# Expert weights in blocks of 256 rows by 1024 columns: two sums from each block, another order of small steps, and a table moved to the third expert

## The chip, the cores and the metric

The kernel runs on one core of one Trainium2 chip. The metric is the device time of one execution in microseconds (us). The time before is 1823.71 us, the median of three runs (1822.42 to 1827.42).

## The reference

The program is one layer of a trunk: a token mixer (Fourier groups beside retention heads), then an expert feed-forward stage, then a last normalisation. The change lies in the expert stage:

```
logits = h @ router_w + router_b            # 1024 tokens, 32 experts
top_vals, top_idx = top_k(logits, 4)
gates = softmax(top_vals)
for each expert e, over the tokens xb that chose it:
    hb    = xb @ w1[e] + b1[e]              # w1[e]: 1024 x 2048, float32
    x_glu = minimum(hb[:, ::2], 7)
    x_lin = clip(hb[:, 1::2], -7, 7)
    act   = x_glu * sigmoid(1.702 * x_glu) * (x_lin + 1)
    out   = act @ w2[e] + b2[e]             # w2[e]: 1024 x 1024
y[token] += gate * out
```

The weights of all 32 experts are 403 MB of float32, read once.

## The kernel before

The mixer takes the first part of the span; from about 540 us on the expert stage runs, and behind it the tail (normalisation of the sums).

**Experts and blocks.** Experts are ordered by load. CAPS[r] is the number of token columns n reserved for rank r; large and small ones alternate (132, 130, 134, 128, 136, ... 176, 91, 192, 84). Experts with n above 128 have two row blocks of tokens, of 128 and n - 128 rows. A weight matrix is cut into blocks of 512 rows by 512 columns (1 MB). An expert has twelve, and twelve steps t = 0 to 11, one block each. q = 0 to 3 are the column quarters of w1, q = 4 and 5 the halves of w2, s = 0 and 1 the upper and the lower 512 rows. The order is (0,0), (0,1), (1,0), (1,1), (2,0), (2,1), (3,0), (3,1), (4,0), (5,0), (4,1), (5,1).

**A step.** `block` (L1418) issues the block's load on SyncE's queue into one of ten `raw` tiles (NRAW). `lower` (L1426) computes on VectorE the remainder of each weight against its upper 16 bits and puts it, as float16, into one of six `lo` tiles (NLO). `product` (L1435) issues 48 matrix products of n columns: 32 with the upper halves of `raw` ("the upper part"), then 16 with `lo` ("the lower part"). The step of u issues `lower` for block u + 4 (AHEAD) and the load of block u + 10, which takes the buffer that step u has freed.

**The small steps between.** The loop at L1373 writes the order out by hand. After step u's product come, in this order: the loads, `lower(u + 4)`, the stages of `swiglu` or `yout` that are pending (L1391), the pending `rest` of a row transpose (L1397), and the next piece of `side` (L1398). `swiglu` has three stages with ScalarE and VectorE taking turns: L1479 to L1482, L1486, L1490 to L1492. At t = 8 all its pending stages run at once. `side` is `finish(r - 1)` from t = 0 (results transposed back, L1338 and L1341, then an indirect DMA into `acc`, L1343) and `turn(r + 1)` from t = 7 (the next expert's gathered token rows transposed, L1459). A piece of `turn` writes one of two `px` banks; its `rest` empties the bank with two ScalarE copies (L1464, L1465) and one VectorE remainder (L1466). With n above 128 there are three pieces, so the third needs the first one's bank.

**Selection and routing.** `select` (L1264) makes, in one VectorE instruction, the 0/1 matrix `sel` that picks an expert's tokens; `batch` (L1271) multiplies it with `aux` on TensorE at t = 5 of every even r, for experts r + 2 and r + 3, and VectorE turns the result into row indices (L1290 to L1298). `gather` (L1306) fetches the rows with an indirect DMA on GpSimd's queue. `routing` (L1079) is a generator; its last two parts run at t = 3 and t = 5 of r = 0 and make the table of surplus token blocks (`tab`, `tabi`) that `overflow` reads. With these inputs the loop of `overflow` runs no time.

Of the kernel before, what the change touches and what calls it, by code (L numbers as in the profile page):

```python
# [9 lines left out]
F32 = mybir.dt.float32  # L10
# [27 lines left out]
NRAW, NLO, AHEAD = 10, 6, 4  # L38
# [69 lines left out]
class K:  # L108
# [23 lines left out]
    def build(self):  # L132
        nc, tc, T = self.nc, self.tc, self.T
        with ExitStack() as es:
# [28 lines left out]
            self.tab = dram.tile([128, 4], F32, name="tab")  # L163
            self.tabi = dram.tile([128, 1], I32, name="tabi")
# [912 lines left out]
    def routing(self, rp):  # L1077
# [150 lines left out]
    def experts(self, routing):  # L1228
# [6 lines left out]
        U = [(r, q, s) for r in range(NE) for q, s in STEPS]  # L1235
        raw, low, info, B, X, A, Y, pss = {}, {}, {}, {}, {}, {}, {}, {}
# [4 lines left out]
        def load(u):  # L1241
            r, q, s = U[u]
            if u % 12 == 0:
                reg[r] = nc.sync.value_load(self.eid[0:1, r:r + 1], min_val=0, max_val=NE - 1)
                B[r] = self.es_.tile([128, 24], F32, name="bias", bufs=3)
            raw[u] = self.block(reg[r], q, s)
            if u % 12 == 0:
                nc.sync.dma_start(B[r], self.biasd[:, bass.ds(reg[r], 1), :].rearrange("p a j -> p (a j)"))
# [7 lines left out]
        def lower(u):  # L1256
            if u < len(U):
                low[u] = self.lower(raw[u])
# [95 lines left out]
        sels[0] = select(0, sel)  # L1354
# [6 lines left out]
        sels[1] = select(1)  # L1361
# [11 lines left out]
        for u, (r, q, s) in enumerate(U):  # L1373
# [23 lines left out]
            run(rest)  # L1397
# [20 lines left out]
    def block(self, e, q, s):  # L1418

        src = self.T["expert_w1" if q < 4 else "expert_w2"][0][bass.ds(e, 1)].rearrange("a (k p) n -> (a p) k n", p=128)  # L1420
        c0 = 512 * (q % 4)
        raw = self.wp.tile([128, 4, 512], F32, name="raw", bufs=NRAW)
        self.nc.sync.dma_start(raw, src[:, 4 * s:4 * s + 4, c0:c0 + 512])
        return raw

    def lower(self, raw):  # L1426

        lo = self.wp.tile([128, 4, 512], F16, name="lo", bufs=NLO)
# [5 lines left out]
    def product(self, ps, raw, lo, s, x, n, pairs):  # L1434


        nc = self.nc
        if pairs:

            up = raw.bitcast(BF).rearrange("p k (c m g h) -> p k c g m h", c=2, g=2, h=2)[:, :, :, :, :, 1]  # L1440
            dn = lo.rearrange("p k (c m g) -> p k c g m", c=2, g=2)
        else:
            up = raw.bitcast(BF).rearrange("p k (c g m h) -> p k c g m h", c=2, g=2, h=2)[:, :, :, :, :, 1]
            dn = lo.rearrange("p k (c g m) -> p k c g m", c=2, g=2)
        for w, parts in ((up, (0, 1)), (dn, (2,))):
            for c in range(2):
                for g in range(2):
                    o = ps[:, c, g * n:g * n + n]
                    for k in range(4):
                        for i in parts:  # L1450
                            nc.tensor.matmul(o, w[:, k, c, g, :], x[:, 4 * s + k, i, :], start=not (s or i or g or k), stop=s == 1 and i == 2 and k == 3, skip_group_check=True)  # L1451
# [52 lines left out]
    def expert(self, n, e, fetched, bias):  # L1504
# [3 lines left out]
        def sums(q, x):  # L1508
            ps = self.ph.tile([128, 2, 512], F32, name="ph")
            for s in range(2):  # L1510
                raw = self.block(e, q, s)
                self.product(ps, raw, self.lower(raw), s, x, n, q < 4)
            return ps

        act = self.ep.tile([128, 8, 3, n], F16, name="act", bufs=1)
        for q in range(4):
            for st in self.swiglu(sums(q, xT), q, act, n, bias):
                st()
        yT = self.ep.tile([128, 8, n], F32, name="yT", bufs=1)
        for q in range(4, 6):  # L1520
            for st in self.yout(sums(q, act), 4 * (q - 4), yT, n, bias):
                st()
# [30 lines left out]
    def overflow(self):  # L1553
# [3 lines left out]
        with tc.For_i(0, cnt, 1) as b:  # L1557
            par = self.es_.tile([128, 4], F32, name="par")
            nc.sync.dma_start(par, self.tab[bass.ds(b, 1), :].to_broadcast([128, 4]))
            ei = self.es_.tile([1, 1], I32, name="ei")  # L1560
            nc.sync.dma_start(ei, self.tabi[bass.ds(b, 1), :])
# [40 lines left out]
```

## Time and profile before

| | us |
|---|---|
| median of three runs | 1823.71 |
| the profiled execution | 1822.8 |
| its span, first to last instruction | 1820.9 |
| TensorE busy in the span | 1693.6 |
| VectorE busy | 1489.6 |
| ScalarE busy | 654.6 |
| GpSimd busy | 252.0 |

The profile is of one execution. Times in its rows count from the start of the span. PE is TensorE's matrix products, PEld its weight loads, DVE is VectorE, ACT ScalarE, POOL GpSimd, SP SyncE. An instruction's idle time stands behind it in brackets with what ended it. The DMA share is the mean busy share of the 16 DMA engines; it goes a little over 1 where packets overlap. PEclk is the granted TensorE clock: 1.00 is 2.4 GHz, 0.50 is 1.2 GHz.

### The profile page before, as it was taken

The page shows a single profiled execution, that of the slowest core. Times are in us where ns is not written, and L with a number is a line of the kernel's source. Part 1 is how long each engine was busy: PE and PEld are TensorE (multiplying, and loading weights), DVE is VectorE, ACT ScalarE, POOL GpSimd, SP SyncE. Part 2 cuts the span into 40 slices and gives each one's busy share as a digit, 9 for nine tenths or more (in the row PEclk, how much of TensorE's full clock was granted, in tenths as well). Part 3 has the DMA queues.
Part 4 walks back from the last instruction along what each step waited for, and adds up shares of the span by engine and source line. Part 5 has one row for each costly group of instructions (what it writes and reads, how often), then busy time and mean ns, then how long its engine had stood idle before and what let it go on. Part 6 is the DMA issues. An engine that isn't in the chain of part 4 may idle for free. (4 is left out here: it accounts for less than half of the span.)

```text
span 1820.9 us, 52628 instructions
## 1 busy us (share of the span) xinstructions
PE 1693.6 (93%) x22388; PEld 1491.6 (82%) x22433; DVE 1489.6 (82%) x2404; ACT 654.6 (36%) x1706; POOL 252.0 (14%) x152
## 2 busy tenths in 40 slices
PE   6999999999976999999999999999999999999991
PEld 2455776546646999999999999999998999999991
DVE  5787876855668989889898898998989889898882
ACT  6443123343211333334333343433433333333433
POOL 0000001100014230112111111211211111110101
PEclk9999999999987999999999999999999999999996
DMA  9324420214339999999999999999999999999986
GB/s 341 122 85 148 141 91 24 61 64 149 109 114 358 314 373 371 372 360 373 363 364 363 356 368 366 372 357 356 366 366 360 358 353 356 356 352 332 362 283 211
DMA packets 260104, 513.99 MB, mean 282 GB/s; under 512 B 21338, under 2 KB 21934, under 8 KB 259864
## 3 DMA queue, kind: packets, MB, share of 16 engines
q1 hardware_dynamic: 242560, 467.45, 72.5%
q0 software_dynamic: 10976, 34.80, 7.9%
q10 hardware_dynamic: 6328, 8.31, 1.4%
q8 instruction: 178, 2.92, 0.7%
q14 instruction: 62, 0.51, 0.1%
HBM read 478.05 MB, written 32.46 MB: 280 GB/s over the span
## 5 line engine op out<-in xcount | busy, mean ns | idle before, releaser
L1431 DVE CUSTOM_DVE_ANT_0 lo<-raw 128x2048 f16<-128x2048 f32 x384 | 870.2, 2284 | 16.7 <-DMA raw<-in_expert_w_dram 10.6
L1451 PEld LDWEIGHTS <-raw 128*128 128x128 bf16 x12288 | 754.5, 109 | 4.0 <-issue 1.7
L1451 PE MATMUL ph<-xT,raw 128*128 128x128 f16 (+25 forms) x8192 | 523.4, 222 | 0.3 <-DVE xT L1466 0.3
L1451 PEld LDWEIGHTS <-lo 128*128 128x128 f16 x6144 | 374.6, 98 | 2.0 <-issue 2.0
L1451 PE MATMUL ph<-xT,lo 128*128 128x128 f16 (+25 forms) x4096 | 279.9, 221 | 0.4 <-issue 0.4
L1451 PE MATMUL ph<-act,raw 128*128 128x128 f16 (+25 forms) x4096 | 270.0, 225 | 0.7 <-DVE act L1492 0.5
L1343 POOL DMA_INDIRECT acc<-orow,idx x49 | 132.7, 2709 | 744.4 <-ACT orow L1341 502.9
L1490 ACT ACTIVATE act<-lin 128x256 f16<-128x256 f32 (+25 forms) x128 | 54.4, 425 | 378.0 <-DVE lin L1486 364.5
L263 PE MATMUL mm<-u 128*128 128x512 f32 x512 | 147.9, 424 | 1.9 <-ACT u L525 1.9
L1479 ACT ACTIVATE lin<-ph,bias 128x128 f32<-128x128 f32 (+25 forms) x256 | 80.2, 364 | 183.3 <-PE ph L1451 181.1
L1451 PE MATMUL ph<-act,lo 128*128 128x128 f16 (+25 forms) x2048 | 141.8, 222 | 1.3 <-issue 1.2
L1500 ACT ACTIVATE yT<-ph,bias,m5s 128x128 f32<-128x128 f32 (+25 forms) x256 | 97.5, 462 | 121.7 <-PE ph L1451 121.7
L263 PE MATMUL mm<-u,h 128*128 128x512 bf16 x488 | 127.3, 391 | 2.8 <-DVE h L527 1.1
L1309 POOL DMA_INDIRECT rows<-Hd,idx x49 | 84.2, 1718 | 285.2 <-PE px L1459 153.8
L263 PE MATMUL mm<-h,u 128*128 128x512 bf16 x491 | 121.7, 379 | 1.5 <-issue 0.6
L263 PEld LDWEIGHTS mm<-u 128*128 128x128 f32 x512 | 95.7, 191 | 28.1 <-ACT u L525 4.8
L263 PEld LDWEIGHTS <-h 128*128 128x128 bf16 x512 | 45.7, 99 | 60.6 <-issue 14.5
L263 PEld LDWEIGHTS <-u 128*128 128x128 bf16 x512 | 48.8, 98 | 55.6 <-issue 1.7
L1341 ACT ACTIVATE orow<-px,inf 128x512 f32<-128x512 f32 (+25 forms) x98 | 67.6, 692 | 71.6 <-PE px L1338 71.6
L1481 ACT ACTIVATE glu<-ph,bias 128x128 f32<-128x128 f32 (+25 forms) x256 | 81.2, 376 | 0.0
L1459 PE MATMUL px<-misc,rows 128*128 128x128 f32 (+25 forms) x392 | 50.0, 254 | 30.8 <-DVE xT L1466 28.1
L1466 DVE SCALAR_TENSOR_TENSOR xT<-px,xT 128x512 f16<-128x512 f32 (+17 forms) x81 | 48.0, 592 | 26.0 <-ACT xT L1465 25.1
(278 smaller groups left out, 1533.5 us busy)
## 6 DMA issues: line engine op xcount, KB each, us to landing
raw<-in_expert_w_dram SPq DMA_DIRECT2D x384, 1024.0 KB
u<-in_mod_w_dram SPq DMA_DIRECT2D x96, 256.0 KB
u<-in_w_in_dram SPq DMA_DIRECT2D x40, 256.0 KB
u<-in_x_dram SPq DMA_DIRECT2D x16, 256.0 KB
u<-in_w_out_dram SPq DMA_DIRECT2D x16, 256.0 KB
u<-in_x_dram ACTq DMA_DIRECT2D x16, 256.0 KB
acc<-u SPq DMA_DIRECT2D x16, 256.0 KB
Hd<-u SPq DMA_DIRECT2D x16, 256.0 KB
```

What stands on the lines that cost most here:

```text
L263: nc.tensor.matmul(ps, l, r, start=i == 0, stop=i == 3 * n - 1)
L1309: nc.gpsimd.indirect_dma_start(out=rows[r, b][0:m, :], out_offset=None, in_=self.Hd, in_offset=bass.IndirectOffsetOnAxis(ap=idx[0:m, :], a ...
L1341: nc.scalar.activation(out[b][0:m, h * 512:(h + 1) * 512], ps[0:m].rearrange("p a n -> p (a n)"), AF.Copy, scale=gate[0:m, :])
L1343: nc.gpsimd.indirect_dma_start(out=self.acc, out_offset=bass.IndirectOffsetOnAxis(ap=idx[0:m, :], axis=0), in_=out[b][0:m, :], in_offset=N ...
L1431: self.nc.vector.tensor_tensor_reduce(flat(lo), flat(raw), flat(raw).bitcast(BF)[:, 1::2], LIFT, 0.0, OP.subtract, OP.max, most)
L1451: nc.tensor.matmul(o, w[:, k, c, g, :], x[:, 4 * s + k, i, :], start=not (s or i or g or k), stop=s == 1 and i == 2 and k == 3, skip_group ...
L1459: nc.tensor.transpose(ps[:, k - k0, 0:m], rows[0:m, k * 128:(k + 1) * 128], self.ident[0:m, 0:m])
L1466: nc.vector.scalar_tensor_tensor(lo, src, SX, hi, op0=OP.mult, op1=OP.subtract)
L1479: nc.scalar.activation(lin[:, c, 0:n], ps[:, c, n:2 * n], AF.Identity, scale=1.0 / SX, bias=bias(8 + 2 * q + c))
L1481: nc.scalar.activation(glu[:, c, 0:n], ps[:, c, 0:n], AF.Silu, scale=ALPHA / SX, bias=bias(2 * q + c))
L1490: nc.scalar.activation(hi, lin[:, :, 0:n], AF.Copy, scale=SA)
L1500: self.nc.scalar.activation(yT[:, j, :], ps[:, i // 2, i % 2 * n:i % 2 * n + n], AF.Identity, bias=bias(16 + j), scale=self.m5s[:, j:j + 1])
```

## The change

A block is now 256 rows by 1024 columns, still 1 MB, in a tile [128, 2, 1024]. An expert has three groups of four blocks: the two column halves of w1, and w2. Each block is used by two quarters: step (q, s) uses blocks 4*(q // 2) + 2*s and the one after it (`used`). So blocks 0 and 1 serve steps 0 and 2, blocks 2 and 3 steps 1 and 3, blocks 4 and 5 steps 4 and 6, 6 and 7 steps 5 and 7, 8 and 9 steps 8 and 9, 10 and 11 steps 10 and 11. A buffer is freed after the last of its two steps (`last`), two at a time. The matrix products and their number are the same. `lower` still runs for block u + 4 at step u, over as many elements; there are eight `lo` tiles instead of six.

The pending `rest` of a row transpose runs ahead of `lower(u + 4)` and of the stages, instead of behind them.

`select` of all experts but the first two runs on GpSimd, as eight instructions, one for each 128 tokens; it is issued at t = 0 instead of t = 6. For experts 2 and 3 it stands behind `gather(1)` in GpSimd's queue.

The last two parts of `routing` run at t = 3 and 5 of r = 2. The second of them ends with a transpose of the table on TensorE, a ScalarE copy and one DMA; the second table `tabi` is gone.

```diff
-NRAW, NLO, AHEAD = 10, 6, 4
+NRAW, NLO, AHEAD = 10, 8, 4
...
-        nc.scalar.dma_start(self.tab, tb)
-        tbi = rp.tile([128, 1], I32, name="tbi")
-        nc.vector.tensor_copy(tbi, tb[:, 2:3])
-        nc.scalar.dma_start(self.tabi, tbi)
+        tbt = self.px.tile([128, 4, 128], F32, name="px")
+        nc.tensor.transpose(tbt[0:4, 0, :], tb, ident)
+        tbr = rp.tile([4, 128], F32, name="tbr")
+        nc.scalar.activation(tbr, tbt[0:4, 0, :], AF.Copy)
+        nc.scalar.dma_start(self.tab, tbr)
...
+        used = lambda u: [u - u % 12 + 4 * (U[u][1] // 2) + 2 * U[u][2] + i for i in range(2)]
+        last = {v: u for u in range(len(U)) for v in used(u)}
...
-        def select(r, sel=None):
+        def select(r, engine=nc.gpsimd, sel=None):
...
+            if engine is nc.gpsimd:
+                for t in range(NT):
+                    engine.tensor_scalar(sel[:, t, 0:w], self.places[:, 0:w], self.prk[:, t, r:r + 1], None, op0=OP.is_equal)
+                return sel
...
-            self.product(ps, raw.pop(u), low.pop(u), s, X[r] if q < 4 else A[r], n, q < 4)
-            freed.add(u)
+            self.product(ps, [raw[v] for v in used(u)], [low[v] for v in used(u)], q % 2, s, X[r] if q < 4 else A[r], n, q < 4)
+            for v in used(u):
+                if last[v] == u:
+                    del raw[v], low[v]
+                    freed.add(v)
             loads()
+            run(rest)
             lower(u + AHEAD)
...
-            run(rest)
             if side and t not in (0, 6):
                 rest.append(side.pop(0)())
...
-            if r == 0 and t in (3, 5):
+            if r == 2 and t in (3, 5):
                 next(routing)
...
-            if t == 6 and r + 4 < NE:
+            if t == 0 and r + 4 < NE:
                 sels[r + 4] = select(r + 4)
...
-        raw = self.wp.tile([128, 4, 512], F32, name="raw", bufs=NRAW)
-        self.nc.sync.dma_start(raw, src[:, 4 * s:4 * s + 4, c0:c0 + 512])
+        raw = self.wp.tile([128, 2, 1024], F32, name="raw", bufs=NRAW)
+        self.nc.sync.dma_start(raw, src[:, 2 * b:2 * b + 2, c0:c0 + 1024])
```

## Rows read from the trace of the kernel before

**Rows 1.** Windows: us, busy of five engines (instructions), PEclk, DMA share, GB/s.

```profile
600.00:650.00 50.00, 48.18 (x782) 47.69 (x779) 44.89 (x58) 21.09 (x58) 9.71 (x5) 0.97 1.05 378
...
800.00:850.00 50.00, 49.93 (x834) 49.60 (x832) 45.38 (x64) 19.32 (x52) 10.50 (x4) 1.00 1.05 375
...
1600.00:1650.00 50.00, 47.25 (x814) 46.97 (x812) 45.87 (x55) 20.02 (x56) 9.66 (x4) 0.97 1.04 359
```

**Rows 2.** Waits of PE, 600 to 1780 us: total, times, longest, in us.

```profile
PE px L1459 <- DVE xT L1466: 27.1, 14, 4.5
```

**Rows 3.** Waits of DVE in the same stretch.

```profile
DVE inf L1290 <- PE px L1283: 43.3, 14, 4.5
DVE xT L1466 <- ACT xT L1465: 23.9, 30, 0.9
DVE lin L1482 <- ACT lin L1479: 19.3, 17, 2.1
```

**Rows 4.** Timeline of PE around one such wait: start, us, instruction.

```profile
1233.30 0.61 PE L1459 MATMUL px<-misc,rows 128*128 128x128 f32 x4
...
1235.32 0.95 PE L1451 MATMUL ph<-act,lo 128*128 128x112 f16 x16
1238.79 0.72 PE L1459 MATMUL px<-misc,rows 24*128 24x24 f32 x8 [2.52 <-DVE xT L1466]
```

**Rows 5.** Timeline of DVE there.

```profile
1233.06 2.28 DVE L1431 CUSTOM_DVE_ANT_0 lo<-raw 128x2048 f16<-128x2048 f32 x1
...
1236.80 0.39 DVE L1492 SCALAR_TENSOR_TENSOR act<-lin,act 128x224 f16<-128x224 f32 x1 [0.46 <-ACT act L1490]
1238.05 0.69 DVE L1466 SCALAR_TENSOR_TENSOR xT<-px,xT 128x512 f16<-128x512 f32 x1 [0.86 <-ACT xT L1465]
```

**Rows 6.** Window behind it, columns as in the first group.

```profile
1239.00:1243.00 4.00, 4.00 (x50) 3.95 (x49) 4.00 (x4) 0.55 (x2) 0.00 (x0) 0.57 1.08 282
```

**Rows 7.** Groups by line of DVE, 600 to 1780 us: count, busy, mean ns, idle.

```profile
L1431 DVE CUSTOM_DVE_ANT_0 lo<-raw 128x2048 f16<-128x2048 f32 x372 | 843.1, 2284 | 16.7 <-DMA raw<-in_expert_w_dram 10.6 <-PE ph L1451 5.1 <-DVE lin L1482 0.5
...
L1268 DVE TENSOR_TENSOR sel<-rows,prk 128x1312 bf16<-128x1312 f32 (+12 forms) x27 | 39.0, 1445 | 0.0
```

**Rows 8.** Timeline of the first expert (PE, DVE, POOL) and a window there.

```profile
578.23 0.60 PE L1150 MATMUL px<-R,ecol 32*128 32x32 f32 x2 [8.15 <-DVE ecol L1148]
...
566.10 2.44 DVE L1268 TENSOR_TENSOR sel<-rows,prk 128x1072 bf16<-128x1072 f32 x2
...
560.37 18.33 POOL L1309 DMA_INDIRECT rows<-Hd,idx  x1 [0.30 <-issue]
...
573.00:584.00 11.00, 5.77 (x51) 5.74 (x52) 10.25 (x19) 1.78 (x6) 5.71 (x1) 0.53 0.97 349
```

**Rows 9.** Timeline at t = 5 of the first expert: batch, then the table on DVE.

```profile
587.19 1.03 PE L1283 MATMUL px<-aux,sel 128*128 128x6 bf16 x32
...
587.29 0.19 DVE L1168 COPY cumi<-px 128x32 f32<-128x32 f32 x1 [2.34 <-PE px L1165]
...
589.19 0.06 DVE L1182 MEMSET tb<- 128x1 f32 x1
```

**Rows 10.** POOL's groups by line, whole span; then timeline of POOL and DVE.

```profile
L1094 POOL CAST aux<-cols 128x256 bf16<-128x256 f32 x1 | 1.2, 1184 | 0.0
...
L355 POOL CAST tri<-misc 128x128 bf16<-128x128 f32 x1 | 0.3, 292 | 2.9 <-DMA misc<-const_misc 2.9
...
632.99 2.64 POOL L1343 DMA_INDIRECT acc<-orow,idx  x1 [8.56 <-DMA acc<-orow,idx]
...
634.27 0.42 DVE L1486 SCALAR_TENSOR_TENSOR lin<-glu,lin 128x260 f32<-128x260 f32 x1
```

**Rows 11.** Timeline of the fourth expert: a remainder on DVE, a lower part on PE.

```profile
687.01 2.29 DVE L1431 CUSTOM_DVE_ANT_0 lo<-raw 128x2048 f16<-128x2048 f32 x1
...
690.41 1.06 PE L1451 MATMUL ph<-xT,lo 128*128 128x128 f16 x16
```

**Rows 12.** DMA of 600 to 1750 us; then one window of the tail.

```profile
DMA packets 206252, 415.96 MB, mean 362 GB/s; under 512 B 12428, under 2 KB 12428, under 8 KB 206068
...
1800.00:1802.00 2.00, 0.00 (x0) 0.00 (x0) 1.27 (x3) 1.15 (x2) 0.55 (x1) 0.50 1.05 416
```

More of the change, by code (lines that the diff above doesn't have):

```diff
@@ L1241, in load @@
         def load(u):
-            r, q, s = U[u]
-            if u % 12 == 0:
+            r, b = u // 12, u % 12
+            if b == 0:
                 reg[r] = nc.sync.value_load(self.eid[0:1, r:r + 1], min_val=0, max_val=NE - 1)
                 B[r] = self.es_.tile([128, 24], F32, name="bias", bufs=3)
-            raw[u] = self.block(reg[r], q, s)
-            if u % 12 == 0:
+            raw[u] = self.block(reg[r], b // 4, b % 4)
+            if b == 0:
                 nc.sync.dma_start(B[r], self.biasd[:, bass.ds(reg[r], 1), :].rearrange("p a j -> p (a j)"))
@@ L1353, in experts @@
         loads(2)
-        sels[0] = select(0, sel)
+        sels[0] = select(0, nc.vector, sel)
         inf = batch([0], [sels[0]], 0, 3)
@@ L1360, in experts @@
         lower(0)
-        sels[1] = select(1)
+        sels[1] = select(1, nc.vector)
         for st in turn(0):
@@ L1416, in experts, with block @@
             st()()
-    def block(self, e, q, s):
-        src = self.T["expert_w1" if q < 4 else "expert_w2"][0][bass.ds(e, 1)].rearrange("a (k p) n -> (a p) k n", p=128)
-        c0 = 512 * (q % 4)
-        raw = self.wp.tile([128, 4, 512], F32, name="raw", bufs=NRAW)
-        self.nc.sync.dma_start(raw, src[:, 4 * s:4 * s + 4, c0:c0 + 512])
+    def block(self, e, h, b):
+        src = self.T["expert_w1" if h < 2 else "expert_w2"][0][bass.ds(e, 1)].rearrange("a (k p) n -> (a p) k n", p=128)
+        c0 = 1024 * (h % 2)
+        raw = self.wp.tile([128, 2, 1024], F32, name="raw", bufs=NRAW)
+        self.nc.sync.dma_start(raw, src[:, 2 * b:2 * b + 2, c0:c0 + 1024])
         return raw
     def lower(self, raw):
-        lo = self.wp.tile([128, 4, 512], F16, name="lo", bufs=NLO)
+        lo = self.wp.tile([128, 2, 1024], F16, name="lo", bufs=NLO)
         most = self.es_.tile([128, 1], F32, name="most", bufs=2)
@@ L1432, in lower, with product @@
         return lo
-    def product(self, ps, raw, lo, s, x, n, pairs):
+    def product(self, ps, raw, lo, h, s, x, n, pairs):
         nc = self.nc
[L1438 to L1444, printed above, removed]
+        spec = "c m g" if pairs else "c g m"
+        up = [r.bitcast(BF)[:, :, 1024 * h:1024 * h + 1024].rearrange(f"p k ({spec} h) -> p k c g m h", c=2, g=2, h=2)[..., 1] for r in raw]
+        dn = [r[:, :, 512 * h:512 * h + 512].rearrange(f"p k ({spec}) -> p k c g m", c=2, g=2) for r in lo]
         for w, parts in ((up, (0, 1)), (dn, (2,))):
@@ L1450, in product @@
                         for i in parts:
-                            nc.tensor.matmul(o, w[:, k, c, g, :], x[:, 4 * s + k, i, :], start=not (s or i or g or k), stop=s == 1 and i == 2 and k == 3, skip_group_check=True)
+                            nc.tensor.matmul(o, w[k // 2][:, k % 2, c, g, :], x[:, 4 * s + k, i, :], start=not (s or i or g or k), stop=s == 1 and i == 2 and k == 3, skip_group_check=True)
     def turn(self, rows, xT, span, b, m):
@@ L1506, in expert, with sums @@
         xT, blocks = fetched
[L1508 to L1513, printed above, removed]
+        def sums(h, x):
+            raw = [self.block(e, h, b) for b in range(4)]
+            lo = [self.lower(r) for r in raw]
+            for g in range(2):
+                ps = self.ph.tile([128, 2, 512], F32, name="ph")
+                for s in range(2):
+                    self.product(ps, raw[2 * s:2 * s + 2], lo[2 * s:2 * s + 2], g, s, x, n, h < 2)
+                yield ps
         act = self.ep.tile([128, 8, 3, n], F16, name="act", bufs=1)
-        for q in range(4):
-            for st in self.swiglu(sums(q, xT), q, act, n, bias):
-                st()
+        for h in range(2):
+            for g, ps in enumerate(sums(h, xT)):
+                for st in self.swiglu(ps, 2 * h + g, act, n, bias):
+                    st()
         yT = self.ep.tile([128, 8, n], F32, name="yT", bufs=1)
-        for q in range(4, 6):
-            for st in self.yout(sums(q, act), 4 * (q - 4), yT, n, bias):
+        for g, ps in enumerate(sums(2, act)):
+            for st in self.yout(ps, 4 * g, yT, n, bias):
                 st()
@@ L1558, in overflow @@
             par = self.es_.tile([128, 4], F32, name="par")
-            nc.sync.dma_start(par, self.tab[bass.ds(b, 1), :].to_broadcast([128, 4]))
+            nc.sync.dma_start(par, self.tab.rearrange("a b -> b a")[bass.ds(b, 1), :].to_broadcast([128, 4]))
             ei = self.es_.tile([1, 1], I32, name="ei")
-            nc.sync.dma_start(ei, self.tabi[bass.ds(b, 1), :])
+            nc.vector.tensor_copy(ei, par[0:1, 2:3])
             oh = self.es_.tile([128, NE], F32, name="oh")
```

3 lines of the change are left out of this document (1 added, 2 removed).

## The prediction

> **What bounds the kernel now.** I read the windows first. From 600 us on TensorE is busy 47 to 50 us of every 50, VectorE about 45, and the DMA share stands at 1.04 or 1.05 [rows 1]. Three engines are near their limit, so the question is which one waits. The waits of TensorE answer it: nearly all of its idle time in the expert stage is one wait, 27.1 us in 14 pieces, of a row transpose for a VectorE remainder [rows 2]. The timeline shows the mechanism: TensorE ends product 9 of a small expert at 1236.27 (1235.32 + 0.95) and stands until 1238.79 [rows 4]. The third transpose needs the first one's bank, and VectorE reaches that bank's remainder only at 1238.05, behind `lower` and the `swiglu` stages, then waiting 0.86 us for ScalarE [rows 5]. Each longer stop costs a second time: right behind this one the granted clock is 0.57 over 4 us [rows 6], so most of that stretch ran at 1.2 GHz and not at 2.4. Seven 50 us windows have a mean of 0.97; the first and the last are shown [rows 1]. Each has lost 0.03 x 50 = 1.5 us, together 10.5 us. VectorE itself waits for TensorE at the `batch` of every even expert, 43.3 us in 14 pieces [rows 3]: there it has caught up, and between two batches it falls behind in the small expert.
>
> The first expert has a stop of its own: 8.15 us at 578.23, TensorE waiting for a VectorE copy of the surplus table that is queued behind remainders; the clock is 0.53 over 573 to 584 [rows 8].
>
> **The change part by part.** The base is the profiled execution, 1822.8 us (span 1820.9 and 1.9 around it), 0.9 us under the median of the runs.
>
> *Bank emptied first.* `rest` now stands ahead of `lower` and of the stages. In the example the remainder at 1238.05 would come before the `lower` at 1233.06 [rows 5], some 4 us earlier, against a stop of 2.52. The longest stop is 4.5 [rows 2]. What is late next is the last `act` remainder of the same expert, which step 10 reads: it ended at 1237.19 (1236.80 + 0.39) [rows 5], and without the stop step 10 would begin about 0.7 us behind 1236.27, one transposes' time [rows 4]. It also has the moved remainder (0.69 us) ahead of it now, so if VectorE gains nothing else some of the stops come back as 0.2 to 2.6 us. I keep 3 of 27.1: **-24** (bounds -27 and -18). ScalarE's copies in `finish` also go ahead of the `swiglu` stages and can delay VectorE's clamp by one copy; that falls in the large experts, ahead of the batch where VectorE waits anyway [rows 3], so nothing.
>
> *Clock.* Of 10.5 us I keep 2: **-8.5** (0 to -10.5).
>
> *Table in the third expert.* The 8.15 us go, and the lost clock, 0.47 x 11 = 5.2 us [rows 8]: -13.3. Two things take it back. Steps 0 and 1 now need two remainders each, the fourth instead of the second before step 1 ends: two instructions of 2.28 us [rows 7], 0 to 4.6, I take 3. And `batch` of experts 2 and 3, in before at 587.19 [rows 9], would come 10.3 us earlier, at 576.9, and needs `sel` from GpSimd. There `gather(1)` held the queue from 560.37 to 578.70; less the two selections that VectorE no longer runs (2.44), 576.3 [rows 8]. Then 16 selections: at 0.29 us each (a GpSimd copy of 128 x 128) 4.7 us, so TensorE would wait about 4; at 0.6 us 9. I take 5, and 3 for the clock behind it. Together -13.3 + 3 + 8 = **-2.3** (-10 to +5). In r = 2 the last part costs something new: the transpose of the table waits on TensorE's queue for VectorE's chain of small instructions, 587.29 to 589.25, 2.0 us [rows 9]; behind it are `batch` and product 6. With a possible clock loss and one bank to be emptied at t = 3: **+4** (+2 to +6). The second table's DMA and cast stood on ScalarE's queue and VectorE beside products: nothing.
>
> *Selection on GpSimd.* VectorE loses 27 instructions, 39.0 us [rows 7], off the path except where it lags. GpSimd gets 8 a rank, 224 in all for the ranks from 4 on, and no row shows one. Bounds: 0.29 us (copy, 128 x 128) and 1.18 us (strided cast of 256 columns) [rows 10]; I take 0.35, near the first, whose shape is nearest. The trace shows that the two engines get in each other's way: GpSimd's indirect DMA from 632.99 ends only 1.4 us behind the end of a running `lower`, when a short VectorE instruction starts at 634.27 [rows 10], and the one from 560.37 took 18.33 us while VectorE ran remainder after remainder [rows 8]. So a selection may wait for a `lower`, and a `lower` for a selection. What GpSimd takes from VectorE is at most 8 x 0.35 = 2.8 us an expert, against 1.4 saved: 2.8 a pair of experts in sum. VectorE's waits in a pair are (43.3 + 23.9 + 19.3) / 14 = 6.2 us [rows 3], which cover it. Uncovered parts, and GpSimd's own queue (the DMAs into `acc` and the gathers stand behind the selections): **+6** (0 to +28).
>
> The Trainium skill has a rule that speaks against this part: SBUF — State Buffer, "Who interferes with whom", says that a VectorE instruction with two SBUF inputs and a GpSimd instruction that reads SBUF exclude each other, the first holding the shared port to its end. `lower` has two such inputs. By that rule the whole 8 x 28 x 0.35 = 78 us would be taken from VectorE, 39 us more than it saves. The trace agrees as far as the 18.33 us go; none of its rows has GpSimd hold up VectorE.
>
> *Blocks.* A descriptor moves 4 KB in place of 2. The stage moved 415.96 MB in 1150 us, 362 GB/s, in packets of 2 KB almost all [rows 12]; without stops and lost clock it would last 1150 - 37.6 = 1112 us and need 374 GB/s, which is the best window of before, 375 [rows 1]. In the tail, where rows of 4 KB are read back, the rate is 416 [rows 12]. So the larger piece pays only by keeping DMA from being next: nothing in the sum. The price is shorter leads. Buffers come free two at a time, after the second use: a load has 3 to 5 steps before its `lower`, in place of 5. And remainders are needed up to two steps earlier: the tightest is block 3 behind a small expert, ready at 689.30 and in before not read until step 3; now step 1's lower part, at 690.41, reads it [rows 11]. 1.1 us remain, and a selection less ahead of it. **+2** (0 to +10).
>
> Sum: -24 - 8.5 - 2.3 + 4 + 6 + 2 = -22.8; 1822.8 - 22.8 = **1800 us**.
>
> **The rivals.**
>
> *GpSimd turns against VectorE (slower).* Place: the small expert's steps, between two batches. At p us a selection VectorE loses 16p - 2.9 a pair; its waits cover 6.2, and the pair grows from p = 0.57 on. From p = 0.70 on the whole change is slower: (16 x 0.70 - 2.9 - 6.2) x 14 = 29 us, what the sum without its GpSimd term (1794) has gained. At p = 0.8 it is 9.9 - 6.2 = 3.7 a pair, x 14 = 52 us, and 1794 + 52 gives **1846**. For it: the 18.33 us, the 1.18 us. Against it: the 0.29 us.
>
> *DMA stays the bound.* If the larger pieces move no faster and the shorter leads let the queue run dry now and then, the stage keeps its 362 GB/s and its 1150 us: only the first expert's -2.3 and the +4 remain, about **1824**. For it: a share of 1.05 in every window [rows 1]; against it: the 416 [rows 12].
>
> The Trainium skill, DMA: Bandwidth & Descriptors, "Specifications", gives about 358 GB/s as the limit of one core's HBM traffic; by it the stage could not go under 415.96 / 358 = 1162 us and the time would not fall. The trace differs: 362 over the stage, 416 in the tail.
>
> *Everything hidden.* No contention, no wait for `sel` at the start, all stops and their clock gone: -27 - 10.5 - 10 + 3 = -44.5, **1778**.
>
> **How the numbers follow.** The forecast case (1787 to 1815) 0.50, everything hidden 0.18, DMA the bound 0.13, GpSimd against VectorE 0.19. Two in ten are left out when the range ends at 1774 below, the last gain beyond the third rival, and at 1836 above, inside the slower rival. A measurement of this kernel tells 0.3% (5.5 us) from no change. Faster by more: 0.50 + 0.18, 0.68, less what of the forecast case ends high: 0.67. Within 0.3%: the DMA case, 0.13. Slower: 0.20.
>
> **What would show it.** After: the wait of `px` L1459 for `xT` under 6 us, and the windows at 0.97 gone; no stop at the first expert's `ecol`, but one at its `batch`; a stop of about 2 us in r = 2 at t = 5; `lower` unstretched at 2.28 us or, for the slower rival, stretched or spaced out beside GpSimd; a DMA rate over 375 GB/s in the stage. I am wrong if GpSimd's queue runs so late that gathered rows are missing at a transpose, or if TensorE waits for `lo` in step 1.

## The result, and the profile after

The changed kernel takes 1802.62 us (median of four runs, 1801.17 to 1804.31) against 1825.47 us for the kernel before (four runs, 1822.42 to 1827.42): a ratio of 0.9877, 95% interval 0.9866 to 0.9889, so 22.9 us less. The profiled execution is the one of 1801.17 us, span 1799.3. The forecast was 1800.

Windows of the stage, columns as in [rows 1]:

```profile
600.00:650.00 50.00, 50.00 (x836) 49.56 (x834) 43.78 (x54) 21.07 (x60) 35.32 (x14) 1.00 0.98 349
650.00:700.00 50.00, 47.62 (x772) 46.76 (x770) 44.28 (x80) 17.80 (x49) 41.50 (x22) 0.97 0.97 357
...
1350.00:1400.00 50.00, 47.86 (x816) 47.29 (x814) 45.33 (x51) 19.81 (x55) 39.23 (x16) 0.97 1.01 369
...
1600.00:1650.00 50.00, 49.94 (x744) 49.63 (x743) 41.27 (x63) 19.03 (x52) 6.05 (x5) 1.00 1.02 373
```

The first column behind the length is TensorE: 50.00 of 50, in most of these windows, where [rows 1] had 47 to 48 at both ends. Of the 23 such windows between 600 and 1750 us two have a granted clock of 0.97 (the second and third shown) and all others 1.00; before there were seven. GpSimd, the fifth engine, now works 25 to 42 us of 50 until the selections end. DMA's share has come down from 1.04 or 1.05 to about 1.02. So TensorE is what bounds the stage now, with DMA close behind.

Waits of TensorE, 600 to 1760 us (total, times, longest):

```profile
PE px L1183 <- DVE tb L1181: 2.1, 1, 2.1
PE ph L1457 <- ACT act L1496: 2.0, 3, 0.8
PE ph L1457 <- DVE act L1498: 1.9, 5, 1.1
...
```

`px` for `xT` (now lines 1465 and 1472), 27.1 us in [rows 2], is gone from this list; the two lines left out are 0.3 and 0.2 us, of other waits. What is left is 3.9 us for `act` (ScalarE's copy and VectorE's remainder), and one stop of 2.1 us for the table. From 540 us on one larger stop is new:

```profile
PE px L1289 <- POOL sel L1272: 10.2, 16, 4.1
```

Waits of VectorE, 600 to 1760 us:

```profile
DVE xT L1472 <- ACT xT L1471: 51.3, 51, 5.2
DVE lo L1440 <- DMA raw<-in_expert_w_dram: 18.6, 27, 2.0
...
DVE inf L1296 <- PE px L1289: 15.9, 11, 3.3
```

The wait at `batch`, 43.3 us in [rows 3], is 15.9; the one ahead of a remainder, 23.9 there, is 51.3, since the remainder now comes first and waits for ScalarE's copy of the same transpose. Both are waits of an engine that is not the bound.

The main groups by line of VectorE (600 to 1760 us) and GpSimd (whole span), then `lower`'s durations by tile (minimum, median, maximum in ns):

```profile
L1440 DVE CUSTOM_DVE_ANT_0 lo<-raw 128x2048 f16<-128x2048 f32 x373 | 852.9, 2308 | 21.5 <-DMA raw<-in_expert_w_dram 18.6 <-PE ph L1457 1.4 <-PE px L1344 0.6
```
```profile
L1272 POOL TENSOR_SCALAR sel<-rows,prk 128x164 bf16<-128x164 f32 (+13 forms) x240 | 525.6, 2203 | 1.2
```
```profile
L1440 DVE CUSTOM_DVE_ANT_0 lo<-raw x384: 2270/2282/2702, 552.6 to 1750.4; 128x2048 f16<-128x2048 f32 x192
```

`lower` has a mean of 2308 ns where [rows 7] had 2284, and its median is 2282: VectorE pays 24 ns x 384 = 9 us in all. A selection on GpSimd has a mean of 2203 ns.

DMA of 620 to 1720 us, and the weight queue's packets, MB and share of time; first of before over the same 1100 us, then of after:

```profile
DMA packets 197016, 397.50 MB, mean 361 GB/s; under 512 B 11935, under 2 KB 11935, under 8 KB 196839
q1 hardware_dynamic: 186887, 363.24, 91.7%
```
```profile
DMA packets 111010, 406.80 MB, mean 370 GB/s; under 512 B 12253, under 2 KB 12257, under 8 KB 110829
q1 hardware_dynamic: 100741, 372.12, 88.6%
```

The weight queue moves 2.4% more bytes in a smaller share of the time: 372.12 / 88.6 = 4.20 MB for each hundredth of it, against 3.96, 6% more. The same figure, over the same stretch, is 3.93 to 3.98 in all five kernels of this document with pieces of 2 KB and 4.05 to 4.20 in all eight with pieces of 4 KB: it goes with the piece.

**Where the time went**, by the start of each expert's first product in the two profiled executions, after against before: the first expert starts 1.8 us later (the stage ahead of it, which the change does not touch; over the kernels below this start scatters from 1.8 earlier to 4.4 later), the second 2.3 later, so the first expert lost 0.5. The fourth starts 6.8 later, so the two between lost 4.5, with the table in the third. From there the difference falls: -0.1 at the eleventh, -8.7 at the nineteenth, -15.1 at the 25th, -22.4 at the end of the products, 29.2 from the fourth expert on. The end of the program is 21.6 earlier.

### The profile page after: what moved, and what is told of

It reads as the page before. It is cut to its first block, busy times and chain, and to the rows that moved or that the text cites. A ratio compares the mean times of both kernels' runs of the same rounds, so it can differ in the third digit from the quotient of the medians.

```text
span 1799.3 us, 52827 instructions
## 1 busy us (share of the span) xinstructions
PE 1691.6 (94%) x22434; PEld 1484.6 (83%) x22434; DVE 1464.8 (81%) x2373; ACT 651.6 (36%) x1707; POOL 765.4 (43%) x392
## 5 line engine op out<-in xcount | busy, mean ns | idle before, releaser
L1440 DVE CUSTOM_DVE_ANT_0 lo<-raw 128x2048 f16<-128x2048 f32 x384 | 877.6, 2307 | 21.5 <-DMA raw<-in_expert_w_dram 18.6
L1272 POOL TENSOR_SCALAR sel<-rows,prk 128x164 bf16<-128x164 f32 (+13 forms) x240 | 525.6, 2203 | 1.2
L1457 PE MATMUL ph<-act,raw 128*128 128x128 f16 (+25 forms) x4096 | 263.3, 221 | 4.1 <-ACT act L1496 2.0
L1349 POOL DMA_INDIRECT acc<-orow,idx x49 | 126.3, 2578 | 278.2 <-DMA acc<-orow,idx 110.3
L1315 POOL DMA_INDIRECT rows<-Hd,idx x49 | 78.5, 1602 | 211.8 <-PE px L1465 114.4
L262 PE MATMUL mm<-u,h 128*128 128x512 bf16 x512 | 132.1, 391 | 0.9 <-DVE h L526 0.9
L121 POOL TENSOR_TENSOR ss<-ss,mhalf 128x1 f32<-128x1 f32 x26 | 15.8, 608 | 259.2 <-DVE ss L120 227.8
L1470 ACT ACTIVATE xT<-px 128x512 f16<-128x512 f32 (+17 forms) x81 | 41.5, 512 | 168.6 <-PE px L1465 168.6
L121 POOL TENSOR_TENSOR v<-v,mhalf 128x8 f32<-128x8 f32 x8 | 14.3, 1785 | 198.9 <-DVE v L120 198.9
```

What stands on the lines that cost most here:

```text
L121: nc.gpsimd.tensor_tensor(out, out, self.mhalf[:, 0:out.shape[1]], op=OP.pow)
L262: nc.tensor.matmul(ps, l, r, start=i == 0, stop=i == 3 * n - 1)
L1272: engine.tensor_scalar(sel[:, t, 0:w], self.places[:, 0:w], self.prk[:, t, r:r + 1], None, op0=OP.is_equal)
L1315: nc.gpsimd.indirect_dma_start(out=rows[r, b][0:m, :], out_offset=None, in_=self.Hd, in_offset=bass.IndirectOffsetOnAxis(ap=idx[0:m, :], a ...
L1349: nc.gpsimd.indirect_dma_start(out=self.acc, out_offset=bass.IndirectOffsetOnAxis(ap=idx[0:m, :], axis=0), in_=out[b][0:m, :], in_offset=N ...
L1457: nc.tensor.matmul(o, w[k // 2][:, k % 2, c, g, :], x[:, 4 * s + k, i, :], start=not (s or i or g or k), stop=s == 1 and i == 2 and k == 3 ...
```

## The experiments

All ratios are against the kernel before, run beside it on the same chip; a difference to the changed kernel is that of the two ratios, times 1825 us.

### One part alone: the bank first

```diff
             loads()
+            run(rest)
             lower(u + AHEAD)
...
-            run(rest)
```

> The kernel before with one edit: the pending rest of a row transpose runs ahead of lower and of the stages. Order theory (the stop was the bank's remainder queued behind lower and stages): the wait of px L1459 for xT falls from 27.1 us to under 6, the clock dips behind it go, the first expert's 8.15 us stop stays, and the time falls by 27 to 36 us, to about 0.982 of before. Rival 1 (VectorE simply lags, and only taking the selection off it helps): the wait stays above 15 us and under 12 us are gained. Rival 2 (DMA at 2 KB pieces is the bound behind the stop): the stops go, but as much comes back as waits of lower for raw, and under 10 us are gained.

Measured: 0.9951 (0.9933 to 0.9968), 1817.12 us: 9 us less, a quarter of what the stops and their clock came to (27.1 + 10.5), and far short of what my theory expected. Waits of TensorE, then of VectorE, 600 to 1760 us:

```profile
PE ph L1451 <- DVE act L1492: 12.0, 25, 1.7
PE ph L1451 <- ACT act L1490: 6.2, 10, 0.9
...
PE px L1459 <- DVE xT L1466: 0.5, 1, 0.5
```
```profile
DVE lo L1431 <- DMA raw<-in_expert_w_dram: 30.3, 47, 2.4
```

The stop for `xT` is gone, as the edit says. In its place TensorE waits 18.2 us for `act`, and `lower` waits nearly three times as long for weights as in [rows 7]. The timeline of TensorE at the place where the kernel before had a stop of 4.46 us, the window behind it, and one `lower` of VectorE ahead of it:

```profile
1388.41 0.69 PE L1459 MATMUL px<-misc,rows 36*128 36x36 f32 x8 [0.50 <-DVE xT L1466]
...
1390.91 0.43 PE L1451 MATMUL ph<-act,raw 128*128 128x108 f16 x3 [1.66 <-DVE act L1492]
1391.99 0.25 PE L1451 MATMUL ph<-act,raw 128*128 128x108 f16 x1 [0.66 <-ACT act L1490]
```
```profile
1391.00:1395.00 4.00, 3.18 (x34) 2.88 (x34) 2.59 (x5) 2.23 (x6) 0.00 (x0) 0.50 1.05 306
```
```profile
1385.16 2.29 DVE L1431 CUSTOM_DVE_ANT_0 lo<-raw 128x2048 f16<-128x2048 f32 x1 [1.46 <-DMA raw<-in_expert_w_dram]
```

The transposes now start 0.50 us late, and step 10, behind them, waits 1.66 and 0.66 for `act`. VectorE had stood 1.46 us for weights ahead of that `lower`, and from there it worked without a pause until the `act` remainder for which step 10 waits: up to 1.46 of the 1.66 us come from the weights. The clock still falls to 0.50, the level of 1.2 GHz: over the stage the windows of this run have lost 10 us to it, as many as before. The stop was mostly moved one step on. It is what rival 2 said: the stop goes, about as much comes back through `lower`'s waits for weights, and under 10 us are gained.

### One part alone: the selections on GpSimd

```diff
+            if pool:
+                for t in range(NT):
+                    nc.gpsimd.tensor_scalar(sel[:, t, 0:w], self.places[:, 0:w], self.prk[:, t, r:r + 1], None, op0=OP.is_equal)
+                return sel
...
-            if t == 6 and r + 4 < NE:
-                sels[r + 4] = select(r + 4)
+            if t == 0 and r + 4 < NE:
+                sels[r + 4] = select(r + 4, pool=True)
```

> The kernel before with one edit: the selections for ranks 4 to 31 on GpSimd, eight instructions each, at t = 0. Order theory: VectorE gains 2 x 1.4 us a pair of experts and loses little to GpSimd (lower 2.28 to 2.31 us), so the remainder comes 2.2 us earlier and the 27.1 us of stops shrink to 4 to 9: 18 to 28 us gained with the clock. Rival 1: the same. Rival 3 (GpSimd takes back from VectorE what it saves): the stops stay at 20 us or more and the time within 0.4% of before.

Measured: 0.9968 (0.9957 to 0.9978), 1820.10 us, 6 us less. TensorE, then VectorE:

```profile
PE px L1463 <- DVE xT L1470: 25.9, 11, 5.7
```
```profile
DVE lo L1435 <- DMA raw<-in_expert_w_dram: 34.3, 46, 2.7
```

The stop keeps its size, though VectorE has 39 us less to do [rows 7]: VectorE used its time to reach `lower` sooner and to wait there for weights, 34.3 us. The size is that of rival 3, its mechanism is not: `lower` has a mean of 2303 ns here, 19 more than in [rows 7], which is 7 us in all. Where the 6 us come from these rows don't show.

### One part alone: the blocks

```diff
-NRAW, NLO, AHEAD = 10, 6, 4
+NRAW, NLO, AHEAD = 10, 8, 4
...
-        raw = self.wp.tile([128, 4, 512], F32, name="raw", bufs=NRAW)
-        self.nc.sync.dma_start(raw, src[:, 4 * s:4 * s + 4, c0:c0 + 512])
+        raw = self.wp.tile([128, 2, 1024], F32, name="raw", bufs=NRAW)
+        self.nc.sync.dma_start(raw, src[:, 2 * b:2 * b + 2, c0:c0 + 1024])
```

> The kernel before with one edit: blocks of 256 rows by 1024 columns, two sums from each, eight lo tiles. Order theory: the stops of 27.1 us stay within 6 us, the rate in the stage stays that of the products, the first expert starts up to 5 us later, and the time is within 0.3% of before. Rival 2 (DMA was the bound): at least 15 us gained, with fewer stops because the pieces come faster. Third case (the shorter leads cost): waits of lower for raw or of PE for lo grow by over 10 us and the time by over 0.4%.

Measured: 1.0008 (0.9995 to 1.0020), 1826.03 us: nothing. TensorE, then VectorE:

```profile
PE px L1461 <- DVE xT L1468: 26.8, 15, 2.8
```
```profile
DVE lo L1436 <- DMA raw<-in_expert_w_dram: 5.8, 11, 2.1
```

`lower` waits for weights half as long as in [rows 7], but with TensorE still held by VectorE that is worth nothing. Three parts alone give -0.49%, -0.32% and +0.08%, together -0.73% or 13 us. All of them in one kernel, with the table moved and the first expert's stop for `sel` taken out (the experiment on `sel` in the first expert, below), give -1.81%. How much of this is due to the three parts, without the table and the start, is set out by place further down: from the fourth expert on, 3.4, 2.5 and 0.9 us for each alone, and 29.2 for all.

### One part taken back: the blocks

The changed kernel with blocks of 512 x 512 and six `lo`.

```diff
-        raw = self.wp.tile([128, 2, 1024], F32, name="raw", bufs=NRAW)
-        self.nc.sync.dma_start(raw, src[:, 2 * b:2 * b + 2, c0:c0 + 1024])
+        raw = self.wp.tile([128, 4, 512], F32, name="raw", bufs=NRAW)
+        self.nc.sync.dma_start(raw, src[:, 4 * s:4 * s + 4, c0:c0 + 512])
```

> The changed kernel with blocks of 512 rows by 512 columns, one sum from each, six lo tiles: pieces of 2 KB. DMA theory: waits of lower for raw grow from 18.6 to 30 us and more, PE waits for act of 8 us and more come with them, and the time is 6 to 15 us above the changed kernel, 0.991 to 0.996 of before. Rival (the pieces pay nothing, as on the kernel before, where they alone gave 1.0008): within 4 us of the changed kernel.

Measured: 0.9996 (0.9984 to 1.0007), 1821.06 us. Without the blocks the whole gain is gone, 22 us, more than the 6 to 15 expected. Its DMA of 620 to 1720 us, then TensorE's waits and VectorE's of 600 to 1760 us:

```profile
DMA packets 197623, 398.68 MB, mean 362 GB/s; under 512 B 11964, under 2 KB 11968, under 8 KB 197445
```
```profile
PE ph L1455 <- DVE act L1496: 9.4, 17, 1.6
PE ph L1455 <- ACT act L1494: 8.0, 10, 1.4
```
```profile
DVE lo L1435 <- DMA raw<-in_expert_w_dram: 49.0, 57, 2.7
```

By its numbers it is the rival "DMA stays the bound" of the prediction: 362 GB/s, and a time within 3 us of its 1824. `lower` waits 49.0 us for weights (18.6 in the changed kernel), and TensorE waits 17.4 us for `act`, as with the bank alone.

### Pieces of 2 KB in the new blocks

The changed kernel, each block loaded by two DMAs of half its columns: the same blocks, buffers and order, but pieces of 2 KB.

```diff
-        self.nc.sync.dma_start(raw, src[:, 2 * b:2 * b + 2, c0:c0 + 1024])
+        for i in range(2):
+            self.nc.sync.dma_start(raw[:, :, 512 * i:512 * i + 512], src[:, 2 * b:2 * b + 2, c0 + 512 * i:c0 + 512 * i + 512])
```

> The changed kernel with each block loaded by two DMAs, one of each 512 columns: the same blocks, order and buffers, but pieces of 2 KB. DMA theory (the size of the piece is what pays): the packets of the stage double, the share of the weight queue goes from 88.6 back to 92%, waits of lower for raw grow to 30 us and more, and the time is 6 to 20 us above the changed kernel (the leads are shorter than in the kernel before). Rival (what pays in the blocks is their order, the eight lo tiles or the freed pairs, not the piece): within 4 us of the changed kernel.

Measured: 1.0086 (1.0068 to 1.0103), 1837.87 us: 38 us over the changed kernel, where 6 to 20 were expected, and 16 over the one with small blocks. DMA (620 to 1720 us), VectorE's wait, and a wait of SyncE's queue (both 600 to 1760 us):

```profile
DMA packets 200523, 393.50 MB, mean 358 GB/s; under 512 B 17335, under 2 KB 17339, under 8 KB 200337
```
```profile
DVE lo L1441 <- DMA raw<-in_expert_w_dram: 51.1, 65, 2.5
```
```profile
SPq L1433 <- DMA raw<-in_expert_w_dram: 261.3, 372, 2.8
```

The block's order and its buffers do not save the gain when the pieces are of 2 KB. But the edit does more than cut the pieces: it doubles the DMAs, and SyncE's queue now stands 261.3 us for earlier weight loads, a wait that neither the changed kernel nor the one before has. The DMA share is 1.00 to 1.06 in all windows of 50 us all the same. So this run alone doesn't show what the piece is worth. What speaks for the piece is that it is what this kernel and the one with small blocks have in common, and that the weight queue moved 3.93 MB for each hundredth of its time here and 3.97 there, against 4.20. The 16 us between the two are the price of the shorter leads and of the doubled DMAs together; they were not parted.

### One part taken back: the bank

```diff
             loads()
-            run(rest)
             lower(u + AHEAD)
...
+            run(rest)
```

> The changed kernel with the rest of a row transpose put back behind lower and the stages. Order theory: with selection and pieces of 4 KB kept, the stops of px for xT come back, smaller than 27 us since VectorE is earlier: 8 to 20 us, and with the clock 10 to 25 us more than the changed kernel, 0.993 to 1.001 of before. Rival (DMA theory: the large pieces alone free VectorE, and the order is no longer needed): under 4 us more than the changed kernel, stops under 5 us.

Measured: 0.9929 (0.9907 to 0.9951), 1809.94 us: 9.5 us over the changed kernel. TensorE, then VectorE, 600 to 1760 us:

```profile
PE px L1465 <- DVE xT L1472: 11.3, 9, 2.6
```
```profile
DVE lo L1440 <- DMA raw<-in_expert_w_dram: 34.1, 40, 3.1
```

The stop for `xT` is back with less than half of its 27.1 us. The edit is worth 9 us alone and 9.5 beside the other parts.

### `sel` in the first expert

The changed kernel, with the selections of experts 2 and 3 on VectorE, as before.

```diff
         for r in (2, 3):
-            sels[r] = select(r)
+            sels[r] = select(r, nc.vector)
```

> The changed kernel with one edit: the selections for experts 2 and 3 stay on VectorE, as one instruction each. If the first batch's 10.2 us stop (TensorE waiting for sel from GpSimd) and the half clock behind it are on the path: 10 to 16 us less than the changed kernel, 0.979 to 0.982 of before. Rival: behind that stop VectorE is late anyway (two selections of 1.2 us more in its queue), so TensorE waits for lo or act instead and under 5 us are gained.

Measured: 0.9819 (0.9798 to 0.9840), 1793.43 us: 10 us under the changed kernel. What it avoids stands in the changed kernel's timeline of GpSimd and TensorE, and in the window over it:

```profile
562.15 21.28 POOL L1315 DMA_INDIRECT rows<-Hd,idx  x1 [0.30 <-issue]
583.48 12.54 POOL L1272 TENSOR_SCALAR sel<-rows,prk 128x134 bf16<-128x134 f32 x21
```
```profile
584.17 0.18 PE L1289 MATMUL px<-aux,sel 128*128 128x6 bf16 x1 [4.08 <-POOL sel L1272]
...
593.07 0.66 PE L1289 MATMUL px<-aux,sel 128*128 128x6 bf16 x17 [0.40 <-POOL sel L1272]
```
```profile
580.00:598.00 18.00, 7.83 (x77) 6.45 (x76) 6.63 (x17) 1.78 (x6) 17.95 (x24) 0.62 0.21 74
```

TensorE stands 4.08 us until the gather lets the first selection through, and from there takes one step of its `batch` for each selection, one every 0.6 us. It is busy 7.83 of 18 us, at a mean clock of 0.62. In this run the same window has 15.18 us and 0.91.

### All selections on VectorE

```diff
-        def select(r, engine=nc.gpsimd, sel=None):
+        def select(r, engine=nc.vector, sel=None):
...
-            if t == 0 and r + 4 < NE:
+            if t == 6 and r + 4 < NE:
```

> The changed kernel with all selections on VectorE again, one instruction each at t = 6 (the first batch then no longer waits for GpSimd either, which alone was worth 9 us less). Theory that all three parts are needed (VectorE's lateness at step 10): VectorE has 2.8 us a pair more, waits of PE for act grow from about 4 to 15 us and more, and the time is 2 to 12 us above the changed kernel in spite of the 9. Rival (selection on GpSimd is worth nothing once the bank is emptied first and the pieces are large): the time is 6 to 12 us under the changed kernel, 0.981 to 0.985 of before.

Measured: 0.9862 (0.9840 to 0.9884), 1795.88 us. Against the changed kernel it is not told apart (-0.0015), so neither the theory (2 to 12 us slower) nor the rival (6 to 12 faster) came out. Waits of TensorE, 600 to 1760 us:

```profile
PE ph L1457 <- ACT act L1496: 3.4, 8, 0.7
PE ph L1457 <- DVE act L1498: 3.1, 14, 0.3
```

TensorE waits 6.5 us for `act`, against 3.9 in the changed kernel and not the 15 of the theory, and no window of 50 us from 600 to 1750 is under 1.00. The early bank and the blocks clear most of the stops without GpSimd's help. Against the kernel just above, which has no stop for `sel` either, this one is 0.0043 or 8 us slower, though the two intervals touch. So what the selections of the later experts on GpSimd are worth beside the other parts is not settled (6 us when alone); with those of experts 2 and 3 GpSimd takes 10 back.

### Each GpSimd selection twice

The changed kernel; each selection from the fifth expert on is issued twice.

```diff
-                for t in range(NT):
+                for t in [t for t in range(NT) for _ in range(1 if r < 4 else 2)]:
```

> The changed kernel with each GpSimd selection from rank 4 on issued twice: 448 instructions in place of 224. If GpSimd holds VectorE up only slightly (in the changed kernel lower is 2.31 us instead of 2.28, 0.02 x 12 a expert), the mean of lower goes to 2.33 us, GpSimd's busy time to about 1250 us, and the time rises by under 6 us. Rival (the port rule in full: each selection stops VectorE for its own length, 0.59 us by the spacing at the first batch): 8 x 0.59 = 4.7 us an expert more, beyond VectorE's slack, and 30 us or more above the changed kernel.

Measured: 1.0387 (1.0357 to 1.0416), 1894.50 us: 93 us over the changed kernel. VectorE's largest group (600 to 1860 us), the longest waits of TensorE (600 to 1900 us) and of ScalarE (600 to 1860 us):

```profile
L1440 DVE CUSTOM_DVE_ANT_0 lo<-raw 128x2048 f16<-128x2048 f32 x374 | 851.7, 2303 | 3.9 <-DMA raw<-in_expert_w_dram 3.9
```
```profile
PE px L1465 <- DMA rows<-Hd,idx: 42.6, 10, 8.7
```
```profile
ACT orow L1347 <- DMA acc<-orow,idx: 217.0, 18, 20.9
```

`lower` has the same mean with twice the selections: 2303 ns. It is not held up further. What fails is GpSimd's queue: the gathers stand behind the selections, and TensorE waits 42.6 us for gathered rows; the sums into `acc` stand there too, and ScalarE waits 217.0 us for its `orow` buffers. The size is that of the rival, the mechanism is the other one that the prediction's last paragraph names.

### The table back in the first expert

```diff
-            if r == 2 and t in (3, 5):
+            if r == 0 and t in (3, 5):
```

> The changed kernel with the last two parts of the routing at t = 3 and 5 of the first expert again. If the stop for sel at the first batch (until 593 us) covers what the table costs there, the third expert's 4.5 us are saved and nothing is paid: 2 to 5 us under the changed kernel. Rival (the forecast's step: the table in the first expert costs its own 8.15 us and its clock): 3 to 10 us above the changed kernel.

Measured: 0.9863 (0.9840 to 0.9885), 1796.28 us; against the changed kernel it is not told apart (-0.0014). TensorE's waits, 540 to 700 us:

```profile
PE px L1149 <- DVE ecol L1147: 2.9, 1, 2.9
PE px L1289 <- POOL sel L1272: 2.5, 6, 0.4
```

The stop for the table comes back as 2.9 us, and that for `sel` shrinks from 10.2 to 2.5: the table's time lies in the time for which TensorE would wait for GpSimd anyway.

### The transpose one step later

The kernel with the selections of experts 2 and 3 on VectorE, and the table's transpose at t = 6 in place of 5.

```diff
         nc.vector.memset(tb[:, 3:4], 0.0)
+        yield
+
         tbt = self.px.tile([128, 4, 128], F32, name="px")
...
-            sels[r] = select(r)
+            sels[r] = select(r, nc.vector)
...
-            if r == 2 and t in (3, 5):
+            if r == 2 and t in (3, 5, 6):
```

> The changed kernel with the selections for experts 2 and 3 on VectorE (worth 9 us by the run before) and the table's transpose one step later, at t = 6 of the third expert, when VectorE's chain is done. If the 2.1 us stop for tb and the half clock behind it (3.4 us at 0.5) are on the path: 3 to 4 us less than with the selections alone, about 0.980 of before. Rival: VectorE's chain still ends behind product 6 and a stop of 1 us or more stays there.

Measured: 0.9828 (0.9814 to 0.9843), 1789.98 us (1788.95 to 1792.38). The transpose in the changed kernel, then in this one:

```profile
672.43 0.27 PE L1183 MATMUL px<-misc,tb 128*4 128x128 f32 x1 [2.14 <-DVE tb L1181]
```
```profile
666.02 0.27 PE L1185 MATMUL px<-misc,tb 128*4 128x128 f32 x1
```

The stop is gone, and no window of 50 us from 600 on is under 1.00. What that is worth isn't told apart from the kernel that has the selections on VectorE and keeps the stop (0.9819). With either, the change is worth 1.7 to 1.8%, some 32 us, and not 23; both beat the kernel before and the changed one.

## Why the prediction came out, and where its steps did not

The time is 2.6 us from the forecast. The sum was right, but not its terms: those of the start and of GpSimd had the wrong size or sign, and the largest was put down to one edit where it needs the blocks too. That the total came so near is in part luck: by place, the stage from the fourth expert on gained 4.7 us more than its terms, and what lies ahead of it and behind it cost 5.9 more.

**Bank emptied first, -24 (-27 to -18): failed as the gain of that edit.** The place and the mechanism were right: the stops are gone with the edit alone. But alone it gives 9 us, and without it the change still gives 13. The step that failed is the one on what is late next. The text named the `act` remainder that step 10 reads and gave it 3 us; the run with this edit alone has 18.2 us of it. The estimate counted one delay (the moved remainder, 0.69 us) and let VectorE run freely otherwise; in that run `lower` stands 30.3 us for weights, and the stages of the same expert stand behind it, as the 1.46 us ahead of a stop of 1.66 show in one place.

**Clock, -8.5: held, by the windows, with bank and blocks together.** Seven windows at 0.97 became two: 5 x 1.5 = 7.5 us; without the selections on GpSimd none is left. Alone the bank gave none of it back: in the run with that edit stops of 0.50, 1.66 and 0.66 us, one behind the other, are followed by a granted clock of 0.50 all the same. Of the two windows left, one has the table's stop of 2.14 us and the other three waits for `act` (1.15, 0.78 and 0.21 us).

**Blocks, +2, "nothing in the sum" for the piece: failed.** For the blocks alone +2 was right (+1.5, interval -1 to +4). But the text itself had worked out that the stage without stops needs 374 GB/s and that the best window of before showed 375 (a misreading: the first row of [rows 1] has 378). With so little slack the rate of the 2 KB pieces is the next bound, and the gain of that paragraph belonged to the sum: taking the blocks back costs 22 us, cutting the new blocks into pieces of 2 KB (with twice the DMAs for it) 38. The shorter leads did no harm here: after 600 us no product waits for `lo`, so the 1.1 us of [rows 11] were enough. The rival "DMA stays the bound" has the time of the change without its blocks. A rate over 375, named as a sign, didn't show over the stage: 370. `lower` still waits 18.6 us for weights, but TensorE is busy nearly without a break, so the rate is what TensorE takes. The Trainium skill, DMA: Bandwidth & Descriptors, "Specifications", would have about 358 GB/s as the limit of a core; the trace disagrees, with 370 over 1100 us.

**Selection on GpSimd, +6 (0 to +28): wrong sign.** Its range had no gain in it, and alone it gains 6 (4 to 8); beside the other parts a gain of 8 is not clear of noise. The 39 us that VectorE sheds were called off the path "except where it lags", and were then given no value at all. The price of one was 0.35 us; where VectorE stands idle beside it, it is 0.6 (21 in 12.54 us). In the stage the timelines of GpSimd and VectorE read so:

```profile
1197.54 19.34 POOL L1272 TENSOR_SCALAR sel<-rows,prk 128x156 bf16<-128x156 f32 x8
```
```profile
1204.48 2.39 DVE L1440 CUSTOM_DVE_ANT_0 lo<-raw 128x2048 f16<-128x2048 f32 x1
...
1206.80 2.28 DVE L1440 CUSTOM_DVE_ANT_0 lo<-raw 128x2048 f16<-128x2048 f32 x1
```

Eight selections take 19.34 us, 2.42 each, one for each `lower`; of the two shown one has lost 0.1 us and the other nothing. Over all 384 the longest `lower` is 2.70 us, and the mean is 24 ns longer than before. So the contention of the prediction exists, but the loser is GpSimd, nearly alone. The rival "GpSimd turns against VectorE" supposed that a selection takes its own length from VectorE; at 0.6 us it should have been at work already, and it was not. The rule of the Trainium skill, SBUF — State Buffer, "Who interferes with whom", by which the two exclude each other, agrees with what GpSimd shows (2.42 us for 0.6) and not with what VectorE shows (2.28 to 2.39 us).

**Table and first expert, -2.3: measured +0.5, inside its bounds (-10 to +5), by a longer stop.** The 8.15 us of [rows 8] went and 10.2 us came, where the text took 5 and 3 for the clock. The gather lasted until 583.4 and not 576.3: it began 1.8 later and took 21.28 us, again beside remainder after remainder, against 18.33 in [rows 8]. Each selection took 0.6 us. Both ends were in the text; of 4 and 9 us the value near the smaller was taken. So long as TensorE waits there for GpSimd, moving the table buys nothing; with the selections of experts 2 and 3 on VectorE the first expert is 9.3 us shorter than before. One thing that the text named as a sign of being wrong did come, TensorE waiting for `lo` in step 1 of the first expert:

```profile
568.00 0.98 PE L1457 MATMUL ph<-xT,lo 128*128 128x132 f16 x14 [1.47 <-DVE most L1440]
```

With 0.43 us in step 0 that is 1.9 us, inside the 3 (0 to 4.6) that the text gave steps 0 and 1.

**r = 2, +4: right,** 4.5, with the stop of 2.14 us where it was forecast.

**The sum by place:** 1.8 from the stage ahead, 0.5, 4.5, and -29.2 from the fourth expert on make -22.4 at the end of the products; the tail gives back 0.8, and the span is 21.6 shorter, against 22.8. The text's terms for the part from the fourth expert on were -24 - 8.5 + 6 + 2 = -24.5. The same part, from the start of the fourth expert to the end of the products, in the profiled execution of each kernel, us shorter than before:

| kernel | us |
|---|---|
| bank alone | 3.4 |
| selections alone | 2.5 |
| blocks alone | 0.9 |
| changed kernel | 29.2 |
| the three kernels that differ from it only ahead of the fourth expert | 31.0, 24.9, 29.8 |
| without the selections on GpSimd | 26.7 |
| without the early bank | 19.8 |
| without the blocks | 7.8 |

The four kernels with all three parts span 24.9 to 31.0, which is how well one execution tells. The parts alone add up to 6.8; the bank and the blocks are each needed for the whole, and for the selections it is not shown. "Everything hidden", 1778, was not reached by any kernel: without the stops for `sel` and for the table the time is still 1790.

## What to carry to other kernels

When several engines are near their limit, work out which wait comes next and the one after that, and give each its price in the same currency as the first: here the three edits of the stage are worth 3.4, 2.5 and 0.9 us alone and 25 to 31 together, and the one that was worth nothing alone costs 22 when it is taken back. A computed need (374 GB/s) that comes within 1% of the best shown rate (378) is a bound, not a cover, so an edit that raises the rate belongs in the sum. A move of work to an idle engine is to be priced by that engine's queue: what stands behind it (gathers, sums into memory), what it stands behind (a gather that lasts 21 us), and its own speed beside the other engines. Of the stop of 10.2 us at the first `batch` 4.1 went to the gather ahead and the rest to selections of 0.6 us each; twice the selections held gathers and sums back by so much that the kernel lost 93 us.

## What the chip showed that was not expected

VectorE and GpSimd do not share evenly: beside a `lower` of 2.28 us a GpSimd selection of 0.6 us stretches to 2.2 (mean of all 240, with those of 0.6 among them), while nine in ten `lower` stay at or under 2.39; with twice the selections `lower` kept its mean (2303 against 2308 ns).

Pieces of 4 KB moved 6% more bytes than pieces of 2 KB for the same share of the weight queue's time (4.20 against 3.96 MB per hundredth). The kernels with 2 KB pieces were 22 us (with the small blocks) and 38 us (with two DMAs a block) slower than the changed one; that all of it is due to the piece is not shown.

Three stops of 0.50, 1.66 and 0.66 us, one behind the other, were followed by a granted clock of 0.50, the 1.2 GHz level, as a single stop of 2.5 us was in [rows 4, 6] (0.57).
